# Reordering the first norm: whose features are loaded first, and at which projection slices the tiles of blocks 2 and 3 are made

## The chip, the cores and the metric

One Trainium2 chip, one of its cores. The metric is the device time of one execution in microseconds (us); the kernel before takes 2851.79 us (median of 3 runs, 2849.84 to 2853.08). All arithmetic that is seen here is in float32; a matmul of full precision is made of three, from high and low halves of its operands.

## The reference, cut to what matters

One transformer layer over 2048 tokens of width 1024. Only the beginning of it matters here: the first norm and the projections of the stick-breaking attention that read its result.

```python
mod_all = einsum('bd,lde->lbe', silu(c), ada_w) + ada_b
h = rms_norm(x, norm_g[0]) * (1 + sc_m) + sh_m     # the first norm, modulated
qkv = (h @ w_qkv).reshape(b, s, 3, 16, 64)
for q0 in range(0, s, 128):                        # stick-breaking attention
    z = q[q0:q0+128] @ k[:q0+128].T * scale
    sp = where(mask, softplus(z), 0); rest = reverse_cumsum(sp)
    a = where(mask, exp(z - rest), 0)
    out[q0:q0+128] = a @ v[:q0+128]
x = x + gate * rms_norm(out @ w_o, norm_g[1])      # then a SwiGLU FFN with its own norms
```

## The kernel before, in words

The 2048 tokens are four blocks (0 to 3) of 512, and the 16 heads are eight pairs. `project` (L429) makes keys, queries and values of one pair for one block. A product is eight **slices**, k = 0 to 7, one for each 128 of the 1024 features, and each slice is three matmuls (`mm3`, L169 to L173). The products come in the order keys (t = 1), queries (t = 0), values (t = 2), so "keys k4" below is slice 4 of the keys. `STEPS` (L33) has the steps in order: pair 0 of block 0, pair 1 of block 0 (the parked step), then pair 0 of blocks 1, 2 and 3, then pair 1 and so on. Between the slices `project_to` (L561) and the main loop put the stages of the attention: scores (`z`, L580), two sigmoids (L597, L599), a scan that breaks the sticks (`w`, L609 and L614), a product on GpSimd (`a`, L621), transposes (`t`, L631), a split of the turned tile in high and low (`aT`, L641 on ScalarE, L647 on VectorE), and the product with the values (`o`, L659). The scores have three PSUM buffers: the fourth score tile waits until the scan has read the first. The turned tiles have two.

The **first norm** of blocks 1 to 3 is woven into the projection of the block ahead of each:

- `x_load` (L304) fetches a block's x by tokens, four loads of 512 KB. `x_square` (L322) makes a tile's sum of squares on ScalarE (L162), the mean on VectorE (L164) and the power on GpSimd (L166). `x_spread` (L336) and `x_share` (L342) turn the four columns into a row that all features use.
- `cols_load` (L316) fetches the same block by features from `xt`, four loads of 512 KB (`xc`), two features' tiles in each.
- `first_norm` (L396) makes tile k of a block: `scale_cols` (L361) multiplies by the row, on VectorE for even k (L365) and on GpSimd for odd k (L369), two tiles ahead of the rest; `modulate` (L371) adds the shift and splits. An even tile costs one ScalarE instruction (L376) and one on VectorE (L377). An odd tile costs two on ScalarE (L381, L382) and one on VectorE (L384), or on GpSimd for block 3. After each odd tile the pair is stored (`h_s`, L407), for the other heads.

TensorE, ScalarE, VectorE and GpSimd each run their instructions in the order in which the Python issues them (the manual schedule). SyncE (SP) issues all loads and stores, from one queue whose order the framework's scheduler decides; each DMA also waits until the eighth one ahead of it has landed.

So the places of the calls in the loop over slices are the order of the queues. Before the change: block 3's x is loaded in the parked step's values k0, block 2's features at block 1's keys k0, block 3's features at block 2's keys k0. Block 3's squares stand in block 1's step at queries k2 and k7 and values k1 and k7 (`SQUARE_AT`, L73), and the first four tiles of a block in the step ahead of it at queries k4 and k6 and values k3 and k5 (`NORM_AT`, L75). The other four are made at the first slices of the block's own keys.

Of the kernel before, what the change touches and what calls it, by code (L numbers as in the profile page):

```python
# [69 lines left out]

H2_STEP = 3

SQUARE_AT = [(0, 2), (0, 7), (2, 1), (2, 7)]  # L73

NORM_AT = [(0, 4), (0, 6), (2, 3), (2, 5)]  # L75

LAST_HELD = 30

def f32(ap):
    return ap.bitcast(F32)  # L80
# [22 lines left out]
def hybrid_trunk_kernel(  # L103
# [55 lines left out]
    def rms_scale(pool, src, tag, junk):  # L159

        ssq = pool.tile([P, 1], F32, name=f"{tag}_ssq", tag="rms_ssq", bufs=10)
        nc.scalar.activation(junk, src, AF.Square, accum_out=ssq)  # L162
        ms = pool.tile([P, 1], F32, name=f"{tag}_ms", tag="rms_ms", bufs=4)
        nc.vector.tensor_scalar(ms, ssq, 1.0 / D, EPS, op0=ALU.mult, op1=ALU.add)  # L164
        rstd = pool.tile([P, 1], F32, name=f"{tag}_rstd", tag="rms_rstd", bufs=4)
        nc.gpsimd.tensor_tensor(rstd, ms, mhalf, op=ALU.pow)  # L166
        return rstd
# [136 lines left out]
    def x_load(b):  # L304
        for i in range(4):
            r0 = b * BT + i * P
            if b == 2:
                if i % 2 == 0:
                    pair = att.tile([P, 2, D], F32, name=f"x{b}_{i}", tag="qt", bufs=BUFS["qt"])
                tok = pair[:, i % 2]  # L310
            else:
                tok = att.tile([P, D], F32, name=f"x{b}_{i}", tag="v", bufs=BUFS["v"])
            nc.sync.dma_start(tok, x[r0 : r0 + P])
            x_tiles[b, i] = tok

    def cols_load(b):  # L316
        for m in range(KC // 2):
            cols = att.tile([P, 2, BT], F32, name=f"xc{b}_{m}", tag="kt", bufs=BUFS["kt"])
            nc.sync.dma_start(cols, xt[b - 1, :, 2 * m : 2 * m + 2])
            x_cols[b, 2 * m], x_cols[b, 2 * m + 1] = cols[:, 0], cols[:, 1]  # L320

    def x_square(b, i):  # L322
        if b > 0:
            tok = x_tiles[b, i]
            x_rstd[b, i] = rms_scale(att, tok, f"n0_{b}_{i}", junk=tok)
            return
        xn = att.tile([P, D], F32, name=f"xn{b}_{i}", tag="kt", bufs=BUFS["kt"])
        x_norm[b, i] = xn
        x_rstd[b, i] = rms_scale(att, x_tiles[b, i], f"n0_{b}_{i}", junk=xn)
# [66 lines left out]
    def first_norm(b, k):  # L396
        if b is None or k >= KC:
            return
        if k % 2 == 0:
            ht = att.tile([P, 2, 2, BT], F32R, name=f"ht0_{b}_{k // 2}", tag="ht", bufs=BUFS["ht"])  # L400
            norm_h.setdefault(b, []).extend([ht[:, 0], ht[:, 1]])
            norm_tile[b] = ht
        for ahead in range(0 if k == 0 else k + 2, min(k + 3, KC)):
            scale_cols(b, ahead)
        modulate(norm_h[b][k], b, k)
        if k % 2 == 1:
            nc.sync.dma_start(h_s[b][:, k - 1 : k + 1], f32(norm_tile[b]))  # L407
# [21 lines left out]
    def project(at):  # L429

        p, b = STEPS[at]
        begun = (p, b) == (0, 0)
        early, parked = (p, b) in EARLY, (p, b) == PARKED

        nb = STEPS[at + 1][1] if at + 1 < len(STEPS) and STEPS[at + 1][0] == 0 else None
        if STEPS[at] == (PARKED[0], 1):
            unpark()
        h = norm_h[b] if p == 0 or parked else h_load(p, b)

        def product(t):  # L440
            if begun:
                return first_acc[t]
            w = weights[p, t]
            if parked and t == 1:
                acc = zps.tile([P, BT], F32, name=f"pj{p}_{b}_{t}", tag="z")
            else:
                acc = accps.tile([P, BT], F32, name=f"pj{p}_{b}_{t}", tag="acc")
            ahead = b == NB - 1 and p + 1 < NPAIR
            for k in range(KC):
                if t == 1:  # L450
                    if p == 0:
                        first_norm(b, k + 4)
                    if k == 0 and nb and nb > 1:
                        cols_load(nb)
                    if k == 5 and waiting:
                        waiting.pop()()
                if parked and t == 1 and k % 2 == 0:
                    nc.sync.dma_start(*stores[k // 2])
                if parked and (t, k) == (1, 6):
                    split_early(1, 2, ["whl"])  # L460
                if nb == 1 and t == 1 and k < 4:
                    x_square(nb, k)
                if nb and t == 1 and 2 <= k < 6:
                    x_spread(nb, k - 2)
                if nb == 1 and (t, k) == (2, 0):
                    x_load(3)
                if nb in (1, 2) and (t, k) in SQUARE_AT:
                    x_square(nb + 1, SQUARE_AT.index((t, k)))
                if nb and (t, k) == (0, 1):
                    x_share(nb)  # L470
                if (t, k) in NORM_AT:
                    first_norm(nb, NORM_AT.index((t, k)))
                if ahead and k == 0:
                    load_weights(p + 1, t)
                if ahead and k == 6:
                    split_weights(p + 1, t)
                mm3(acc, (w[0][:, k], w[1][:, k]), (h[k][:, 0], h[k][:, 1]), k == 0, k == KC - 1)
                yield
            return acc

        def split(acc, tag):
            hl = att.tile([P, 2, BT], F32R, name=f"{tag}n{p}_{b}", tag="qkn", bufs=BUFS["qkn"])
            nc.scalar.copy(hl[:, 0], acc)
            nc.vector.tensor_tensor(hl[:, 1], acc, f32(hl[:, 0]), op=ALU.subtract)
            return hl

        closing = (p, b) == (NPAIR - 1, NB - 1)
        if closing:
            wo_load(0, 0, "whl")
            wo_load(0, 1, "ht")  # L490
        n = split((yield from product(1)), "k")
        if closing:
            wo_load(0, 2, "whl")
        if parked:
            nc.sync.dma_start(k_park, f32(n))
        else:
            kt = att.tile([P, 2, BT], F32R, name=f"kt{p}_{b}", tag="kt", bufs=BUFS["kt"])
            for e in range(2):
                for part in range(2):
                    nc.sync.dma_start(  # L500
                        f32(kt[part * HD : (part + 1) * HD, e]), f32(n[e * HD : (e + 1) * HD, part])
                    )
            keys[p, b] = kt

        n = split((yield from product(0)), "q")
        if closing:
            wo_load(0, 3, "whl")
        if parked:
            nc.sync.dma_start(q_park, f32(n))
        else:  # L510
            qt = att.tile([P, 2, 2, BT], F32R, name=f"qt{p}_{b}", tag="qt", bufs=BUFS["qt"])
            for e in range(2):
                for half in range(2):
                    nc.sync.dma_start(
                        f32(qt[half * HD : (half + 1) * HD, e]), f32(n[e * HD : (e + 1) * HD])
                    )
            queries[p, b] = qt

        acc = yield from product(2)
        tag = "w" if early else "tmp"  # L520
        vT = att.tile([P, BT], F32, name=f"vT{p}_{b}", tag=tag, bufs=BUFS[tag])
        nc.scalar.copy(vT, acc)

        def values_turn():
            pool, ptag = (zps, "z") if early else (accps, "acc")
            pt = pool.tile([P, 4, 2, HD], F32, name=f"vt{p}_{b}", tag=ptag)
            for i in range(4):
                nc.tensor.transpose(
                    pt[:, i].rearrange("p e d -> p (e d)"), vT[:, i * P : (i + 1) * P], ident
                )  # L530
            v = att.tile([P, 4, 2, 2, HD], F32R, name=f"v{p}_{b}", tag="v", bufs=BUFS["v"])
            nc.scalar.copy(v[:, :, :, 0], pt)
            nc.vector.tensor_tensor(v[:, :, :, 1], pt, f32(v[:, :, :, 0]), op=ALU.subtract)
            if parked:
                nc.sync.dma_start(v_park, f32(v))
            else:
                values[p, b] = v

        if early:
            waiting.append(values_turn)  # L540
            return
        for _ in range(VGAP):
            yield
        values_turn()
# [911 lines left out]
    for n, (s, f) in enumerate(groups):  # L1456
# [3 lines left out]
        for at, product in enumerate(PRODUCTS):  # L1460
            acc = banks_of[{1: 0, 6: 0, 7: 0, 4: 0, 5: 1, 3: 1, 2: 2}[product]]
            for k in range(H4):
# [4 lines left out]
                t = 4 * at + k  # L1467
# [193 lines left out]
```

## Time and profile before

| what | value |
|---|---|
| median of 3 runs | 2851.79 us (2849.84 to 2853.08) |
| the profiled execution | 2850.27 us |
| its span, first to last instruction | 2848.1 us |
| TensorE busy | 2791.3 us, 98% of the span |
| VectorE / ScalarE / GpSimd busy | 2024.3 / 1636.4 / 1293.5 us |
| mean granted TensorE clock | 0.998 |

The profiled execution's own time is 2850.27 us: 2.2 us of it lie outside the span. Rows of the trace have the start in us from the span's beginning, the duration, the engine, the line of the kernel, the tiles (out<-in), and in brackets the idle time of the engine just before and what ended it. PE is TensorE, DVE VectorE, ACT ScalarE, POOL GpSimd, SPq the queue of SyncE. In rows with three numbers and slashes these are minimum, median and maximum in ns.

### The profile page before, as it was taken

What the parts mean: (1) busy time and instruction counts of PE and PEld (TensorE: products, weight loads), DVE (VectorE), ACT (ScalarE), POOL (GpSimd) and SP (SyncE); (2) the same over time, 40 slices, a digit from 0 to 9 for tenths busy, and PEclk for the clock granted to TensorE, in tenths of its full rate; (3) what the DMA queues carried; (4) which work ended last, traced back from release to release, by engine and by line L of the source; (5) the groups of instructions that cost most, each with busy time, mean ns of one, the idle gap of its engine ahead of it and who ended that gap; (6) DMA issues with size and microseconds to landing.
All of it is one profiled execution on the core that took longest, in us unless ns stands there. A gap on an engine that the chain in (4) does not pass through costs nothing.

```text
span 2848.1 us, 41654 instructions
## 1 busy us (share of the span) xinstructions
PE 2791.3 (98%) x13764; PEld 2327.7 (82%) x13764; DVE 2024.3 (71%) x2817; ACT 1636.4 (57%) x3278; POOL 1293.5 (45%) x2040
## 2 busy tenths in 40 slices
PE   7899999999999999999999999999999999999998
PEld 6688888888888888887888888888788888888887
DVE  6788898888888888888866766655776655133367
ACT  5787877788787877777645533333433333322243
POOL 1575666666575655657410122221222222544454
PEclk9999999999999999999999999999999999999999
DMA  9865546657565635546288644334453335545575
GB/s 367 312 213 172 189 149 233 208 171 235 184 211 193 205 121 179 198 131 232 83 304 308 207 137 152 122 94 160 135 170 115 111 100 171 191 133 154 180 230 187
DMA packets 241095, 523.12 MB, mean 184 GB/s; under 512 B 22512, under 2 KB 110576, under 8 KB 223216
## 3 DMA queue, kind: packets, MB, share of 16 engines
q1 hardware_dynamic: 240880, 520.47, 56.1%
q8 instruction: 108, 1.77, 0.3%
q14 instruction: 107, 0.88, 0.1%
HBM read 353.14 MB, written 118.49 MB: 166 GB/s over the span
## 4 chain that ended last, share of the span: by engine, by line
PE 86%; DVE 5%; DMA 3%; ACT 2%; issue 2%; POOL 1%; SPq 0%; DVEq 0%; ACTq 0%; POOLq 0%
PE s L171 9%; PE s L172 9%; PE s L173 9%; PE z L580 8%; PE o L659 8%; PE t L631 8%; PE pj L171 5%; PE pj L173 5%; PE pj L172 5%; PE o L171 5%; PE o L173 5%; PE o L172 5%; PE y L173 1%; PE y L171 1%; PE y L172 1%
## 5 line engine op out<-in xcount | busy, mean ns | idle before, releaser
L621 POOL TENSOR_TENSOR a<-a,w 128x512 f32<-128x512 f32 (+3 forms) x640 | 619.9, 969 | 211.5 <-DVE w L614 127.1
L614 DVE TENSOR_TENSOR_SCAN w<-z,c,begin 128x512 f32<-128x512 f32 x384 | 489.2, 1279 | 81.7 <-ACT z L599 60.2
L171 PE MATMUL s<-r,l 128*128 128x512 f32 x1232 | 482.2, 391 | 4.3 <-DVE p L1423 3.9
L173 PE MATMUL s<-r,l 128*128 128x512 f32 x1232 | 480.0, 390 | 0.0
L172 PE MATMUL s<-r,l 128*128 128x512 f32 x1232 | 480.0, 390 | 0.0
L597 ACT ACTIVATE a<-z 128x512 f32<-128x512 f32 (+3 forms) x640 | 347.1, 542 | 167.0 <-PE z L580 135.2
L659 PE MATMUL o<-aT,v 128*128 128x512 f32 (+3 forms) x1280 | 384.3, 381 | 0.1
L647 DVE TENSOR_TENSOR aT<-t,aT 128x512 fp32r<-128x512 f32 (+3 forms) x640 | 358.9, 594 | 22.8 <-ACT aT L641 22.2
L580 PE MATMUL z<-kt,qt 128*128 128x512 f32 (+3 forms) x1280 | 363.8, 365 | 6.2 <-DVE w L609 6.2
L641 ACT CAST aT<-t 128x512 fp32r<-128x512 f32 (+3 forms) x640 | 314.3, 534 | 73.5 <-PE t L631 63.5
L599 ACT ACTIVATE z<-z 128x512 f32<-128x512 f32 (+3 forms) x640 | 345.5, 540 | 0.0
L1431 POOL TENSOR_TENSOR one<-p,p 128x512 f32<-128x512 f32 x44 | 71.5, 1624 | 578.6 <-issue 321.9
L171 PE MATMUL pj<-ht,w 128*128 128x512 f32 x768 | 308.8, 402 | 5.7 <-issue 1.4
L631 PE MATMUL t<-begin,a 128*128 128x128 f32 x2176 | 295.2, 273 | 13.4 <-DVE aT L647 10.3
L631 PEld LDWEIGHTS t<-begin,a 128*128 128x128 f32 x2176 | 255.0, 140 | 63.4 <-DVE aT L647 14.1
L172 PE MATMUL pj<-ht,w 128*128 128x512 f32 x768 | 302.8, 394 | 1.6 <-DVE ht L767 0.7
L173 PE MATMUL pj<-ht,w 128*128 128x512 f32 x768 | 302.6, 394 | 0.0
L171 PEld LDWEIGHTS s<-r,l 128*128 128x128 f32 x1232 | 231.5, 188 | 55.2 <-ACT l L1284 2.9
L173 PEld LDWEIGHTS s<-r,l 128*128 128x128 f32 x1232 | 231.7, 188 | 48.2
L172 PEld LDWEIGHTS s<-r,l 128*128 128x128 f32 x1232 | 231.7, 188 | 48.1 <-issue 0.5
L580 PEld LDWEIGHTS z<-kt,qt 128*128 128x128 f32 x1280 | 230.7, 189 | 44.2 <-DVE w L609 7.1
L609 DVE TENSOR_TENSOR_SCAN w<-z,begin 128x128 f32<-128x128 f32 (+3 forms) x256 | 208.7, 818 | 77.8 <-ACT z L599 64.9
(170 smaller groups left out, 4860.7 us busy)
## 6 DMA issues: line engine op xcount, KB each, us to landing
ht<-h_s SPq DMA_DIRECT2D x108, 1024.0 KB, 8.2
wi<-in_win SPq DMA_DIRECT2D x86, 512.0 KB, 3.9
qt<-qn SPq DMA_DIRECT2D x124, 256.0 KB, 4.9
ol_qt<-act_s SPq DMA_DIRECT2D x56, 512.0 KB, 3.8
act_s<-S SPq DMA_DIRECT2D x66, 256.0 KB, 4.0
br<-in_wout SPq DMA_DIRECT2D x66, 256.0 KB, 3.7
h_s<-ht SPq DMA_DIRECT2D x16, 1024.0 KB, 10.2
o_s<-os SPq DMA_DIRECT2D x128, 128.0 KB, 2.7
```

What stands on the lines that cost most here:

```text
L171: nc.tensor.matmul(acc, lhs[0], rhs[0], start=first, stop=False, **kw)
L172: nc.tensor.matmul(acc, lhs[0], rhs[1], start=False, stop=False, **kw)
L173: nc.tensor.matmul(acc, lhs[1], rhs[0], start=False, stop=last, **kw)
L580: nc.tensor.matmul(z[:, :n], q[:, e, part, r * P : (r + 1) * P], k[:, e, :n], start=part == 0, stop=part == 1,)
L597: nc.scalar.activation(a[:, :n], z[:, :n], AF.Sigmoid, scale=QK_SCALE)
L599: nc.scalar.activation(z[:, :n], z[:, :n], AF.Sigmoid, scale=-QK_SCALE)
L614: nc.vector.tensor_tensor_scan(rest[:, rev], left[:, rev], begin[:, :BT][:, rev], initial=carries[r], op0=ALU.mult, op1=ALU.bypass,)
L621: nc.gpsimd.tensor_tensor(a[:, :n], a[:, :n], rest[:, 1 : n + 1], op=ALU.mult)
L631: nc.tensor.transpose(pt[:, rb * P : (rb + 1) * P], weighed[i, rb][:, j * P : (j + 1) * P], ident)
L641: nc.scalar.copy(hl[:, 0, t0:], pt[:, t0:])
L647: nc.vector.tensor_tensor(hl[:, 1, t0:], pt[:, t0:], f32(hl[:, 0, t0:]), op=ALU.subtract)
L659: nc.tensor.matmul(acc[:, t0:], lhs, hl[:, part, t0:], start=sc == qb and j == 0 and part == 0, stop=sc == 0 and j == 3 and part == 1,)
```

## The change

Loads: in the parked step's values k0, block 2's features are loaded in place of block 3's x. Block 3's x is loaded at block 1's keys k0, where block 2's features were. Block 3's features are loaded at block 1's values k0, in place of block 2's keys k0.

Squares: those of block 3 move to block 1's values k0, k2, k4 and k6. Those of block 2 stay.

Tiles: block 1's stay. Of blocks 2 and 3, three tiles (0, 1, 2) are made in the step ahead, at values k2, k4 and k6, and the other five at k0 to k4 of the block's own keys.

```diff
-SQUARE_AT = [(0, 2), (0, 7), (2, 1), (2, 7)]
+SQUARE_AT = {1: [(0, 2), (0, 7), (2, 1), (2, 7)], 2: [(2, 0), (2, 2), (2, 4), (2, 6)]}
 
-NORM_AT = [(0, 4), (0, 6), (2, 3), (2, 5)]
+NORM_AT = {
+    None: [], 1: [(0, 4), (0, 6), (2, 3), (2, 5)],
+    2: [(2, 2), (2, 4), (2, 6)], 3: [(2, 2), (2, 4), (2, 6)],
+}
...
                     if p == 0:
-                        first_norm(b, k + 4)
-                    if k == 0 and nb and nb > 1:
-                        cols_load(nb)
+                        first_norm(b, k + (4 if b == 1 else 3))
+                    if k == 0 and nb == 2:
+                        x_load(3)
...
-                if nb == 1 and (t, k) == (2, 0):
-                    x_load(3)
-                if nb in (1, 2) and (t, k) in SQUARE_AT:
-                    x_square(nb + 1, SQUARE_AT.index((t, k)))
+                if nb in (1, 2) and (t, k) == (2, 0):
+                    cols_load(nb + 1)
+                if nb in (1, 2) and (t, k) in SQUARE_AT[nb]:
+                    x_square(nb + 1, SQUARE_AT[nb].index((t, k)))
                 if nb and (t, k) == (0, 1):
                     x_share(nb)
-                if (t, k) in NORM_AT:
-                    first_norm(nb, NORM_AT.index((t, k)))
+                if (t, k) in NORM_AT[nb]:
+                    first_norm(nb, NORM_AT[nb].index((t, k)))
```

`nb` is the block of the next step, if that step is of pair 0.

## The prediction

> **What bounds the kernel now.** I read the page first, for TensorE's share; then the waits of PE, cut at 150 us; then busy time by stretch, cut where the products begin and end; and last the rows of each engine around the one long gap.
>
> ```profile
> PE 2791.3 (98%) x13764; PEld 2327.7 (82%) x13764; DVE 2024.3 (71%) x2817; ACT 1636.4 (57%) x3278; POOL 1293.5 (45%) x2040
> ```
> ```profile
> PE z L580 <- DVE w L609: 6.2, 1, 6.2
> PE t L631 <- DVE aT L647: 4.2, 4, 1.3
> PE t L631 <- POOL w L594: 1.7, 1, 1.7
> PE vt L528 <- ACT vT L522: 1.3, 1, 1.3
> ```
> ```profile
> 88.50:94.90 6.40, 0.21 (x2) 0.02 (x1) 5.81 (x9) 5.92 (x13) 3.61 (x5) 0.91 1.01 422
> 94.90:98.20 3.30, 1.95 (x6) 1.24 (x7) 1.45 (x4) 3.26 (x8) 3.15 (x5) 0.50 1.05 408
> 98.20:108.60 10.40, 9.76 (x42) 7.25 (x41) 9.15 (x13) 7.28 (x16) 4.76 (x9) 0.89 0.93 297
> 108.60:118.20 9.60, 9.60 (x54) 8.04 (x53) 8.27 (x14) 5.83 (x15) 6.87 (x13) 1.00 0.98 369
> 118.20:130.90 12.70, 10.63 (x55) 8.40 (x54) 11.16 (x15) 12.16 (x26) 8.53 (x14) 1.00 0.80 251
> 136.60:150.00 13.40, 11.14 (x60) 9.06 (x59) 11.17 (x14) 12.24 (x23) 9.02 (x13) 1.00 0.50 186
> 150.00:250.00 100.00, 100.00 (x549) 85.19 (x548) 85.07 (x106) 80.44 (x167) 65.18 (x139) 1.00 0.61 192
> ```
>
> TensorE is the bound for the whole span. The second fence holds its waits from 60 to 150 us (total, times, longest). The stretches (length, then busy PE, PEld, DVE, ACT, POOL, granted clock, DMA share, GB/s) show where: block 1's values end at 88.5, then comes a gap, then block 2's keys from 98.2, queries from 108.6, values from 118.2, block 3's keys from 136.6. From 150 to 250 PE is busy in 100 of 100 us. So whatever the change does must be done before 150, and a shift there reaches the end one for one. What is there to win is small: 6.2 + 1.3 us for the gap, 4.2 + 1.7 in the small waits after it, some slow matmuls behind the gap (clock 0.50 and 0.89). The DMA share is 1.0 until 98: the loads land when bandwidth lets them.
>
> The gap itself:
>
> ```profile
> 78.81 1.06 ACT L162 ACTIVATE x<-x 128x1024 f32<-128x1024 f32 x1 [0.58 <-DMA x<-in_x]
> 79.78 0.19 ACT L162 ACTIVATION_READ_ACCUMULATOR x<-x 128x1 f32 x1
> ```
> ```profile
> 87.02 0.75 DVE L365 SCALAR_TENSOR_TENSOR xc<-xc,g_eff,x 128x512 f32<-128x512 f32 x1 [6.87 <-DMA xc<-in_xt]
> 88.30 1.17 DVE L365 SCALAR_TENSOR_TENSOR xc<-xc,g_eff,x 128x512 f32<-128x512 f32 x1 [0.52 <-DMA xc<-in_xt]
> 89.39 1.75 DVE L377 SCALAR_TENSOR_TENSOR ht<-xc,shift,ht 128x512 fp32r<-128x512 f32 x1
> 94.41 0.42 DVE L609 TENSOR_TENSOR_SCAN w<-z,begin 128x128 f32<-128x128 f32 x1
> ```
> ```profile
> 94.88 1.22 PE L580 MATMUL z<-kt,qt 128*128 128x512 f32 x2 [6.19 <-DVE w L609]
> 97.44 1.11 PE L528 MATMUL vt<-begin,vT 128*128 128x128 f32 x4 [1.35 <-ACT vT L522]
> ```
>
> Block 2's features land at 87.0 and 88.3. VectorE stood at the first of them for 6.87 us, and the sigmoids and the scan of the first attention unit were queued behind. PE's fourth score tile needs that scan (94.41 + 0.42 = 94.83) and starts at 94.88.
>
> **The change part by part.** No instruction is added or taken away, and the build's order shows TensorE's unchanged. Only queues differ.
>
> (1) The loads. Block 2's features go where block 3's x was in SP's queue, and the x where the features were:
>
> ```profile
> L313 SPq DMA_DIRECT2D x<-in_x x4: 1178/1206/1231, 67.5 to 71.4; - x4
> DMA to landing us min/median/max: 11.2/11.5/11.9
> ```
> ```profile
> L319 SPq DMA_DIRECT2D xc<-in_xt x4: 328/328/1167, 74.0 to 78.8; - x4
> DMA to landing us min/median/max: 12.5/12.7/13.0
> ```
>
> Both are four loads of 512 KB with the same DMAs ahead, so they trade landings: the features land by 71.4 + 11.9 = 83.3, the x lands its four tiles at 87.0, 88.3, then at the latest 78.8 + 12.7 = 91.5 (estimates from these rows).
>
> (2) What stands there then. The features are no longer late, but block 3's squares now come first: ScalarE's new order is the split of the queries, squares 0 and 1, the high half of tile 0 (L376), square 2, tile 1 (L381, L382), the first sigmoids. VectorE has both means (L164) ahead of tile 0's scaling, and GpSimd both powers (L166) ahead of tile 1's. So the same sigmoids now stand behind the x's second tile.
>
> ```profile
> L365 DVE SCALAR_TENSOR_TENSOR xc<-xc,g_eff,x x11: 737/749/1557, 60.8 to 125.0; 128x512 f32<-128x512 f32 x11
> L376 ACT ACTIVATE ht<-xc,shift x10: 710/722/786, 61.6 to 123.5; 128x512 fp32r<-128x512 f32 x10
> L369 POOL TENSOR_TENSOR xc<-xc,x x10: 1295/1734/1816, 61.9 to 118.0; 128x512 f32<-128x512 f32 x10
> L377 DVE SCALAR_TENSOR_TENSOR ht<-xc,shift,ht x9: 740/752/1754, 62.3 to 115.3; 128x512 fp32r<-128x512 f32 x9
> L381 ACT ACTIVATE xc<-xc,shift,g_eff x9: 802/813/817, 63.4 to 117.3; 128x512 f32<-128x512 f32 x9
> L382 ACT CAST ht<-xc x9: 618/620/622, 64.2 to 118.1; 128x512 fp32r<-128x512 f32 x9
> L384 DVE TENSOR_TENSOR ht<-xc,ht x8: 659/692/1201, 64.9 to 107.3; 128x512 fp32r<-128x512 f32 x8
> ```
> ```profile
> 93.01 0.15 DVE L164 TENSOR_SCALAR n_ms<-n_ssq 128x1 f32<-128x1 f32 x1 [0.36 <-ACT x L162]
> ```
> ```profile
> 93.31 0.92 POOL L166 TENSOR_TENSOR n_rstd<-n_ms,mhalf 128x1 f32<-128x1 f32 x1 [0.81 <-DVE n_ms L164]
> ```
> ```profile
> 93.66 0.27 ACT L599 ACTIVATE z<-z 128x128 f32<-128x128 f32 x1
> ```
>
> The chain: landing 88.3, square and readout 1.25 (89.55), mean, and power by 0.30 + 0.92 after the mean's start (90.8), L369 1.73 (92.5), L381 0.81 and L382 0.62 (93.9), two sigmoids of 0.27 (94.5). VectorE's L384 0.69 fits beside the sigmoids (94.6), the scan 0.42: 95.0. ScalarE's rows overlap by some 0.1 us each, so 94.6 is as likely. Against 94.83 that is -0.2 to +0.2; with L384 at its longest +0.7. **I take 0: the wait stays and changes its owner**, from the features to the x. Behind it ScalarE has square 3 (1.06), L376 (0.72), two sigmoids and the copy that the values' transposes need, where it now has L381, L382, the same sigmoids, square 3 and that copy: 0.7 less. I take -0.4 for block 2's first key slice, 97.8 instead of 98.2.
>
> (3) Block 2's keys, one tile fewer in stock.
>
> ```profile
> 98.60 0.59 ACT L532 CAST v<-vt 128x512 fp32r<-128x512 f32 x1 [0.43 <-PE vt L528]
> ```
> ```profile
> 101.29 1.21 DVE L609 TENSOR_TENSOR_SCAN w<-z,begin 128x512 f32<-128x512 f32 x1
> ```
> ```profile
> 102.82 0.39 PE L172 MATMUL pj<-ht,w 128*128 128x512 f32 x1
> ```
>
> PE wants the low half of tile 4 at 102.8, less 0.4. VectorE's order puts it behind the fourth scan and a scaling. Ahead of that scan ScalarE now has L381 and L382 after its cast at 98.60, where it had L376: +0.71 against -0.4, within the slack to 101.29. So the scan ends at about 102.4, L365 at 103.1, L377 at 103.9, or 104.9 if it takes its longest 1.75: a wait of 1.4 to 2.4 us at k4. Tile 6 follows over a spread and a scan, 0 to 1.2 more. The present waits at k7, about 0.6, go. With the -0.4: +0.4 to +2.6, and -0.9 if the x lands 1.3 us sooner after its issue, as in its old place. I take **+0.8**, near +0.4, as most L377 are at their median.
>
> (4) Block 2's queries lose tiles 0 and 1 of block 3. PE is busy 9.60 of 9.60 there, so nothing is won inside; but the queues arrive emptier, and two waits of VectorE's splits just behind (about 0.7 of the 4.2) should go: **-0.7**, ends -0.7 and 0.
>
> (5) Block 2's values gain them. ScalarE is busy 12.16 of 12.70 there, and gets L376, L381, L382 and gives one L381, L382 to block 3's keys: +0.72. VectorE gets two L365 and one L377, +2.25. PE's transposes have two buffers that VectorE's splits free.
>
> ```profile
> 127.47 0.55 PE L631 MATMUL t<-begin,a 128*128 128x128 f32 x3 [1.31 <-DVE aT L647]
> 134.97 0.77 PE L631 MATMUL t<-begin,a 128*128 128x128 f32 x5 [1.66 <-POOL w L594]
> ```
>
> Following the new order, the split that frees the second buffer comes some 2 us late near 131, and the wait at 134.97, which now ends with GpSimd, takes in 1.4 of it: **+0.6**, ends 0 and 0.72 + 2.25 = +3.0.
>
> (6) Block 3's keys make five tiles instead of four: ScalarE +1.43 in a stretch where it is busy 12.24 of 13.40; GpSimd +2.6.
>
> ```profile
> 141.34 0.18 POOL L620 COPY c<-w 128x1 f32<-128x1 f32 x1 [4.11 <-DVE w L609]
> ```
>
> GpSimd's part fits into these 4.11 us; ScalarE's doesn't all, and the last low half is behind one more product of GpSimd: **+1.2**, ends 0 and 1.43 + 1.3 = +2.7.
>
> (7) The rest costs nothing. Block 3's features move up, from block 2's keys k0 to block 1's values k0, behind the queries' copies, while their first use moves back into block 2's values: more slack at both ends. Block 2's first store stands behind three of these loads; its buffer is wanted only in block 2's values. Near 131 to 170 the scheduler moves weight loads ahead of stores and of block 3's queries; PE has no wait there. If these covers failed, VectorE would wait for features as it does now at 87.
>
> Sum: 0 + 0.8 - 0.7 + 0.6 + 1.2 = **+1.9 us**. The profiled execution took 2850.27 (span 2848.1 and 2.2 around it), so 2852.2; the median shown is 1.5 higher, so 2853.7 on its scale. The terms' ends that can go together give -2 to +5.
>
> One rule speaks against the change. The Trainium skill, SBUF — State Buffer, "Who interferes with whom", has VectorE instructions with two SBUF inputs and GpSimd instructions that read SBUF lock each other out. The trace agrees: L377 took 1.75 at 89.39, its median being 0.75, while GpSimd scaled tiles. By that rule three more such instructions beside GpSimd would each lose 1.0 us, an estimate that makes the sum +4.9.
>
> **The rivals.**
>
> *A, faster: the first scan is no longer held.* If the x landed by 82, the scan would follow block 1's values at once: 6.2 + 1.3 gone, and up to 2.0 of slow matmuls (half of the 1.95 at clock 0.50, 0.11 of the 9.76 at 0.89), then 1 to 3 given back at block 2's keys, where PE would outrun the tiles: -6.5 to -8.5, so 2843 to 2845. For it: the x landed 1.3 us faster than the features. Against it: that is 1.3 us, not 6, and DMA share is 1.0 on both sides. Chance 0.13. The Trainium skill, TensorE: Matmul & The Clock Gate, Part 1, says that an idle window of about 3.4 us halves the clock; the 0.50 agrees, and by it those matmuls are won only if the gap falls below that.
>
> *B, slower: the splits fall behind in block 2's values.* Terms 3, 5 and 6 at their ends, +2.6 + 3.0 + 2.7 = +8.3, less term 4's 0.7 and what the ends share: +6 to +8, so 2858 to 2860. It decides when a split near 131 is later than the 1.66 us that PE waits anyway, so that each scan starts late and the next unit inherits it. For it: ScalarE's 12.16 of 12.70. Against it: DVE idles 1.5 in that stretch. Chance 0.17.
>
> *C, a small gain.* The x lands 1.3 faster, term 3 is 0 and the waits of term 4 go: -1 to -4, so 2848 to 2851. Chance 0.08.
>
> That the change doesn't do what it says is no rival: SP's order in the build has the loads where the diff puts them.
>
> **How the numbers follow.** My forecast has 0.62, its own range -2 to +5: 2850 to 2857. I call 0.2%, 5.7 us, no change, about what a measurement of this kernel can tell. Forecast and C lie within it: same 0.70; A faster 0.13, B slower 0.17. The range from 2845 to 2860 holds forecast, C and B, 0.87, and reaches A's edge.
>
> **What would show it.** Right: ScalarE's first square of block 3 waits for DMA until about 87, the fourth score tile starts at 94 to 96, a wait for L377 appears at block 2's key k4, PE is full from 150 on. Wrong: a square of block 3 that starts at 79 to 83, a score gap under 3 us (A), or waits on L647 over 6 us between 118 and 150 (B).

## Result, and the profile after

| | before | after |
|---|---|---|
| median | 2852.31 us (2849.27 to 2854.36, 12 runs) | 2858.95 us (2857.17 to 2860.66, 12 runs) |
| span of the profiled execution | 2848.1 us | 2857.2 us |
| mean granted TensorE clock | 0.998 | 0.996 |

The ratio of after to before is 1.0023, interval 1.0014 to 1.0032: between 4.0 and 9.1 us slower. The predicted 2853.7 was 5.2 too low. The range from 2845 to 2860 holds the time, but the forecast's own range, 2850 to 2857, does not: the time lies where only rival B reached. Whether it is more than the 5.7 us that the prediction called no change stays open, as the interval has both.

Line numbers of after are three higher than those of before behind `NORM_AT` (L75). The first two views answer to the prediction's first two: the page's busy times, then TensorE's waits from 60 to 160 us (total, times, longest).

```profile
PE 2795.6 (98%) x13764; PEld 2330.5 (82%) x13764; DVE 2032.9 (71%) x2817; ACT 1638.1 (57%) x3278; POOL 1296.4 (45%) x2040
```
```profile
PE z L583 <- DVE n_ms L167: 8.6, 1, 8.6
PE t L634 <- DVE aT L650: 5.9, 4, 2.3
PE pj L175 <- DVE ht L380: 2.6, 3, 2.2
PE pj L175 <- DVE ht L387: 0.7, 2, 0.4
PE pj L175 <- POOL ht L387: 0.2, 1, 0.2
```

The gap ahead of the fourth score tile is 8.6 us and no longer 6.2. The 1.3 for `vt` and the 1.7 for GpSimd are gone; 2.6 for L380 are new, and the splits cost 5.9 where they cost 4.2. The row names the tiny mean L167 as the one that ended the gap, because it is the instruction that VectorE finished last; what TensorE needed was the scan just before it (below).

**Where the time went.** TensorE's order is the same in both kernels, so the same score tile can be looked up in both, and the distance between two such tiles is free of what an execution lost before. Here are five of them, before and then after. They are a tile of block 1's values, the first in block 2's keys, the first in block 2's values, the first in block 3's keys after slice k0, and one near the end of the disturbed stretch.

```profile
85.87 0.40 PE L580 MATMUL z<-kt,qt 128*128 128x256 f32 x2
...
99.64 0.52 PE L580 MATMUL z<-kt,qt 128*128 128x128 f32 x2
...
119.04 0.68 PE L580 MATMUL z<-kt,qt 128*128 128x512 f32 x2
...
137.59 0.68 PE L580 MATMUL z<-kt,qt 128*128 128x512 f32 x2
...
156.24 0.68 PE L580 MATMUL z<-kt,qt 128*128 128x512 f32 x2
```
```profile
86.08 0.40 PE L583 MATMUL z<-kt,qt 128*128 128x256 f32 x2
...
100.82 0.52 PE L583 MATMUL z<-kt,qt 128*128 128x128 f32 x2
...
122.07 0.68 PE L583 MATMUL z<-kt,qt 128*128 128x512 f32 x2
...
141.90 0.68 PE L583 MATMUL z<-kt,qt 128*128 128x512 f32 x2
...
161.75 0.68 PE L583 MATMUL z<-kt,qt 128*128 128x512 f32 x2
```

The four distances were 13.77, 19.40, 18.55 and 18.65 us; they are 14.74, 21.25, 19.83 and 19.85. So the **gap** costs 0.97 more, block 2's **keys and queries** 1.85, its **values** 1.28, and block 3's **keys** 1.20: 5.30 in all. That lies inside the interval of the medians. The spans differ by 9.1; the other 3.8 arise ahead of the first tile (0.2) and behind the last (3.6, most of it after 2400 us), where the change touches nothing, and single executions of the kernel before differ by 5 us among themselves (2849.27 to 2854.36). So the experiments below are read by these four distances, with the medians as a check.

From there on TensorE is full, as it was from 150 before (length, busy PE, PEld, DVE, ACT, POOL, granted clock, DMA share, GB/s):

```profile
156.00:256.00 100.00, 99.97 (x548) 85.04 (x549) 85.41 (x107) 80.94 (x168) 65.14 (x140) 1.00 0.57 182
```

**The gap.** Rows of ScalarE, GpSimd, VectorE and TensorE of after around it:

```profile
88.42 1.06 ACT L165 ACTIVATE x<-x 128x1024 f32<-128x1024 f32 x1 [5.19 <-DMA x<-in_x]
...
90.22 1.06 ACT L165 ACTIVATE x<-x 128x1024 f32<-128x1024 f32 x1 [0.64 <-DMA x<-in_x]
```
```profile
95.27 1.27 POOL L372 TENSOR_TENSOR xc<-xc,x 128x512 f32<-128x512 f32 x1
```
```profile
95.53 1.56 DVE L387 TENSOR_TENSOR ht<-xc,ht 128x512 fp32r<-128x512 f32 x1 [0.92 <-ACT ht L385]
97.01 0.41 DVE L612 TENSOR_TENSOR_SCAN w<-z,begin 128x128 f32<-128x128 f32 x1
```
```profile
97.47 1.22 PE L583 MATMUL z<-kt,qt 128*128 128x512 f32 x2 [8.57 <-DVE n_ms L167]
```

The wait is where the prediction put it, on the x's first two tiles. But they start at 88.42 and 90.22, not at 87.0 and 88.3. The low half L387 takes 1.56 where its median before was 0.69, beside GpSimd's scaling of a tile. The scan ends at 97.42, not at 95.0.

The view of the two load lines shows why the x is late (issue durations, first and last issue; then DMA to landing, minimum, median, maximum). First the x, then the features:

```profile
L316 SPq DMA_DIRECT2D x<-in_x x4: 327/328/1197, 74.2 to 80.6; - x4
...
DMA to landing us min/median/max: 12.1/14.0/14.3
```
```profile
L322 SPq DMA_DIRECT2D xc<-in_xt x4: 1152/1206/1254, 67.8 to 71.7; - x4
...
DMA to landing us min/median/max: 12.8/12.9/13.1
```

The features need 12.9 us where the x needed 11.5 in the same place, and the x behind them needs 14.0 where the features needed 12.7, with the last issue at 80.6 and not at 78.8. The loads did not trade landings: the second one lost 1.3. Why loads by features take longer than loads by tokens is not shown.

**The values.** Two stretches between the same two score tiles in block 2's values, first before, then after:

```profile
128.09:135.82 7.73, 6.07 (x39) 5.12 (x38) 6.31 (x10) 5.51 (x15) 6.91 (x13) 1.00 0.42 138
```
```profile
130.20:140.13 9.93, 7.65 (x39) 6.51 (x38) 7.91 (x12) 7.36 (x18) 8.26 (x14) 0.83 0.51 182
```
```profile
135.87 0.33 PE L634 MATMUL t<-begin,a 128*128 128x128 f32 x1 [2.28 <-DVE aT L650]
```

The stretch is 2.20 longer. TensorE idles 9.93 - 7.65 = 2.28 in it, all in the one wait of the row, where it idled 1.66: 0.62 more. The other 1.58 are busy time: the same matmuls at a granted clock of 0.83 in place of 1.00.

**Block 3's keys.** Here the sum of the idle time hardly moves (18.65 - 16.39 = 2.26 before, 19.85 - 17.48 = 2.37 after), at a granted clock of 1.00 in both. The starts of the matmuls show the loss. Where slices follow each other without a wait, the starts are 0.23 apart; at two low halves that GpSimd makes they are 0.48 and 0.61 behind the matmul ahead, and the next matmul 0.33 and 0.34 behind them: 0.84 of the 1.20. The second of them:

```profile
154.64 0.39 PE L174 MATMUL pj<-ht,w 128*128 128x512 f32 x1
155.25 0.50 PE L175 MATMUL pj<-ht,w 128*128 128x512 f32 x1 [0.22 <-POOL ht L387]
```

### The profile page after: what moved, and what is told of

It is laid out like the page before. It is cut to its first block, busy times and chain, and to the rows that moved or that the text cites. A ratio compares the mean times of both kernels' runs of the same rounds, so it can differ in the third digit from the quotient of the medians.

```text
span 2857.2 us, 41657 instructions
## 1 busy us (share of the span) xinstructions
PE 2795.6 (98%) x13764; PEld 2330.5 (82%) x13764; DVE 2032.9 (71%) x2817; ACT 1638.1 (57%) x3278; POOL 1296.4 (45%) x2040
## 3 DMA queue, kind: packets, MB, share of 16 engines
q8 instruction: 108, 1.77, 0.3%
## 4 chain that ended last, share of the span: by engine, by line
PE 86%; DVE 5%; issue 3%; ACT 3%; DMA 2%; POOL 1%; SPq 0%; DVEq 0%; POOLq 0%; ACTq 0%
PE s L174 9%; PE s L176 9%; PE s L175 9%; PE z L583 8%; PE o L662 8%; PE t L634 8%; PE pj L174 6%; PE pj L175 5%; PE pj L176 5%; PE o L176 4%; PE o L175 4%; PE o L174 4%; PE y L176 2%; PE y L174 2%; PE y L175 2%
## 5 line engine op out<-in xcount | busy, mean ns | idle before, releaser
L650 DVE TENSOR_TENSOR aT<-t,aT 128x512 fp32r<-128x512 f32 (+3 forms) x640 | 358.9, 595 | 24.0 <-ACT aT L644 23.3
```

The costliest lines, as they stand in the source:

```text
L650: nc.vector.tensor_tensor(hl[:, 1, t0:], pt[:, t0:], f32(hl[:, 0, t0:]), op=ALU.subtract)
```

## The experiments

All by the distances between the five score tiles, as change against before in us, and by medians; each median of before was measured beside that of the run. Each kernel has one trace. In e1, e5, e6 and e10 the four transposes of block 3's row come four slices later on TensorE, within "keys, queries"; elsewhere its order is unchanged.

| kernel | gap | keys, queries | values | block 3's keys | sum | median us, before us | ratio (interval) |
|---|---|---|---|---|---|---|---|
| after | +0.97 | +1.85 | +1.28 | +1.20 | +5.30 | 2858.95, 2852.31 | 1.0023 (1.0014 to 1.0032) |
| e1 | -9.08 | +4.10 | +1.16 | +1.22 | -2.60 | 2848.7, 2851.89 | 0.9990 (0.9981 to 0.9999) |
| e2 | +0.42 | +2.95 | -0.47 | +0.02 | +2.92 | 2855.22, 2851.89 | 1.0013 (1.0004 to 1.0022) |
| e3 | +1.73 | +0.03 | +1.28 | +1.23 | +4.27 | 2856.6, 2851.89 | 1.0018 (1.0009 to 1.0027) |
| e4 | +5.19 | +0.02 | +0.02 | +0.02 | +5.25 | 2857.74, 2851.89 | 1.0020 (1.0011 to 1.0030) |
| e5 | -8.50 | +3.87 | +0.12 | 0.00 | -4.51 | 2848.14, 2852.17 | 0.9986 (0.9977 to 0.9995) |
| e6 | -8.49 | +3.77 | +1.42 | +1.24 | -2.06 | 2848.76, 2852.17 | 0.9987 (0.9978 to 0.9996) |
| e7 | +0.90 | +2.73 | -2.11 | +1.26 | +2.78 | 2852.99, 2852.17 | 1.0002 (0.9993 to 1.0011) |
| e8 | +0.77 | +2.05 | +0.29 | +1.26 | +4.37 | 2857.1, 2852.17 | 1.0015 (1.0006 to 1.0023) |
| e9 | -2.52 | +1.85 | +1.29 | +1.24 | +1.86 | 2854.95, 2851.9 | 1.0011 (1.0002 to 1.002) |
| e10 | -8.50 | +3.77 | +1.13 | +0.01 | -3.59 | 2849.36, 2851.9 | 0.9992 (0.9984 to 1.0001) |

All the sums lie inside the intervals of their ratios. The theory is that the loss has four places that are separate: the x lands late and holds the scan; block 2's keys lack a tile; block 2's values make tiles 0 to 2 of block 3 in place of 2 and 3, with five scalings in place of two; block 3's keys have one tile too many. The main rival puts it in one place, from which the rest is inherited.

**e1: block 3's squares, late.** The loads and tiles stay as changed; the squares go behind the first scans, to block 2's keys k5 and k7 and queries k1 and k2, and the row that is made of them with them.

```diff
-SQUARE_AT = {1: [(0, 2), (0, 7), (2, 1), (2, 7)], 2: [(2, 0), (2, 2), (2, 4), (2, 6)]}
+SQUARE_AT = {1: [(0, 2), (0, 7), (2, 1), (2, 7)], 3: [(1, 5), (1, 7), (0, 1), (0, 2)]}
+
+SPREAD_AT = {1: [(1, 2), (1, 3), (1, 4), (1, 5)], 2: [(1, 2), (1, 3), (1, 4), (1, 5)], 3: [(1, 7), (0, 1), (0, 3), (0, 4)]}
+
+SHARE_AT = {1: (0, 1), 2: (0, 1), 3: (0, 5)}
...
-                if nb and t == 1 and 2 <= k < 6:
-                    x_spread(nb, k - 2)
+                if nb and (t, k) in SPREAD_AT[nb]:
+                    x_spread(nb, SPREAD_AT[nb].index((t, k)))
...
-                if nb in (1, 2) and (t, k) in SQUARE_AT[nb]:
-                    x_square(nb + 1, SQUARE_AT[nb].index((t, k)))
-                if nb and (t, k) == (0, 1):
+                if nb in (1, 3) and (t, k) in SQUARE_AT[nb]:
+                    x_square(2 if nb == 1 else 3, SQUARE_AT[nb].index((t, k)))
+                if nb and (t, k) == SHARE_AT[nb]:
                     x_share(nb)
```

> The changed kernel, with block 3's squares moved behind the first scans (block 2's keys k5 and k7, queries k1 and k2), and their spreads and the row after them (row at queries k5). Theory (the first scan waits for block 3's x, 8.6 us in the changed kernel): the fourth score tile starts by 90 instead of 97.5, and the gap shrinks from 8.6 to under 2 us. Some of it comes back in block 2's keys, whose tiles are made at one per some 1.4 us: 4 to 6 us faster than the changed kernel, 2852 to 2855 when that is at 2859, so level with the kernel before or up to 3 us faster. Rival (bandwidth or the elementwise work of this stretch is the bound, and the order only says where the wait shows): the score gap goes, but block 2's keys end at the same 111 to 112 us as in the changed kernel, and the time stays within 2 us of 2859.

The gap is gone: 4.69 us from the first score tile to the second, at a granted clock of 1.00, where before it took 13.77 at 0.78. The two windows, e1's and then before's:

```profile
85.70:90.39 4.69, 4.47 (x24) 3.52 (x22) 3.60 (x7) 3.97 (x11) 1.47 (x4) 1.00 1.04 422
```
```profile
85.87:99.64 13.77, 6.24 (x24) 4.49 (x22) 9.53 (x15) 10.92 (x22) 8.74 (x12) 0.78 1.02 413
```

Of the 9.08, 1.77 are busy time (6.24 - 4.47), the rest idle time. So the features do land in time, and the squares, which stood waiting for the x, made the gap of after. But 4.10 are given back at once in block 2's keys and queries, where TensorE now waits for low halves:

```profile
93.76 0.50 PE L179 MATMUL pj<-ht,w 128*128 128x512 f32 x1 [1.16 <-DVE ht L391]
...
97.04 0.80 PE L179 MATMUL pj<-ht,w 128*128 128x512 f32 x1 [2.32 <-DVE ht L384]
```

Even so the median, 2848.7, is below the theory's 2852 to 2855: the kernel is faster than after, and just faster than before.

**e2: block 3's tiles at their old places.**

```diff
-    2: [(2, 2), (2, 4), (2, 6)], 3: [(2, 2), (2, 4), (2, 6)],
+    2: [(2, 2), (2, 4), (2, 6)], 3: [(0, 4), (0, 6), (2, 3), (2, 5)],
-                        first_norm(b, k + (4 if b == 1 else 3))
+                        first_norm(b, k + (3 if b == 2 else 4))
```

> The changed kernel with block 3's first four tiles back at their old places (queries k4, k6, values k3, k5; the others four slices ahead). Loads, squares and block 2's tiles stay changed. Theory: the loss behind 118 us (block 2's values and block 3's keys, some 3 us of the 5.3 that stand at 160 us in the profile) goes, the score gap of 8.6 and the wait at k4 of block 2's keys (2.2) stay: 2 to 3 us faster than the changed kernel, about 2856. Rival (the late waits only pass on what the gap lost): no more than 1 us faster.

The losses in block 2's values and in block 3's keys go (-0.47 and +0.02): 2.93 less than in after. The keys and queries lose 1.10 more, ahead of block 3's tiles: the granted clock is 0.91 over them where after has 0.97, and busy time 19.65 where it has 18.45 (what the clock hangs on stands under e8). With 0.55 less in the gap, the sum is 2.4 below after's 5.30.

**e3: four tiles of block 2 ahead**, at block 1's values k1, k3, k5 and k7.

```diff
-    2: [(2, 2), (2, 4), (2, 6)], 3: [(2, 2), (2, 4), (2, 6)],
+    2: [(2, 1), (2, 3), (2, 5), (2, 7)], 3: [(2, 2), (2, 4), (2, 6)],
-                        first_norm(b, k + (4 if b == 1 else 3))
+                        first_norm(b, k + (3 if b == 3 else 4))
```

> The changed kernel with four tiles of block 2 made ahead instead of three (values k1, k3, k5, k7; the others four slices ahead). Theory: the wait of 2.2 us for tile 4's low half at k4 of block 2's keys goes, the score gap stays at 8 to 9.5 us since the first tile's place is only one slice earlier: 1 to 2.5 us faster than the changed kernel. Rival (VectorE's and ScalarE's work there is full, and a tile made earlier holds up the scan as long): the gap grows by what the wait at k4 gives, no difference.

Keys and queries lose nothing any more (+0.03), and the wait for L380 shrinks from 2.6 to this row:

```profile
PE pj L175 <- DVE ht L380: 0.2, 1, 0.2
```

The values' loss stays at 1.28 and block 3's at 1.23, so neither is inherited from block 2's keys. The gap grows by 0.76: ScalarE makes tile 3 (0.80 and 0.62 us) ahead of the copy for the values' transposes, and TensorE waits 2.3 for that copy.

**e4: the loads alone.** The kernel before, with only block 3's x and block 2's features exchanged.

```diff
-                    if k == 0 and nb and nb > 1:
-                        cols_load(nb)
+                    if k == 0 and nb == 2:
+                        x_load(3)
+                    if k == 0 and nb == 3:
+                        cols_load(3)
...
-                    x_load(3)
+                    cols_load(2)
```

> The kernel before with one part of the change: block 2's features are loaded in the place of block 3's x and the x in theirs. Squares and tiles stay at their old places, block 3's features too. Theory (the wait changes its owner): ScalarE now stands on the x at the first square, at queries k2, about 88 to 90, and the score gap is 6 to 9 us: 0 to +4 us against the kernel before. Rival (the features were what was late, and the loads alone cure it): the score gap falls below 3 us and the time by 4 us or more.

+5.25 us, all of it in the gap, more than the theory's range. ScalarE then TensorE:

```profile
90.39 1.06 ACT L162 ACTIVATE x<-x 128x1024 f32<-128x1024 f32 x1 [12.11 <-DMA x<-in_x]
```
```profile
PE z L582 <- DVE w L611: 11.4, 1, 11.4
```

The squares stand at block 1's queries k2 there, so ScalarE stands 12.11 us for an x that lands at 90.4, and everything behind it is late. With the squares ahead of the scan, the exchange takes no wait away; in e1, with the squares behind it, it does.

**e5: e1, with four tiles of block 2 and block 3's tiles near their old places.** This is the version to which e1 to e3 point.

```diff
-    2: [(2, 2), (2, 4), (2, 6)], 3: [(2, 2), (2, 4), (2, 6)],
+    2: [(2, 1), (2, 3), (2, 5), (2, 7)], 3: [(0, 6), (2, 1), (2, 3), (2, 5)],
-                        first_norm(b, k + (4 if b == 1 else 3))
+                        first_norm(b, k + 4)
```

> The version of e1 (loads as changed, block 3's squares late) with four tiles of block 2 made ahead (values k1, k3, k5, k7) and block 3's tiles near their old places (queries k6, values k1, k3, k5). Theory: the three losses are separate and add. e1 took 2848.7; taking a fourth tile of block 2 ahead should be worth the 2.1 us of block 2's keys, block 3's old places the 2.9 us that e2 (2855.2) lay below a changed kernel of 2858.95, less about 1 for the queries: 2844 to 2846, with no wait over 1 us for a low half in block 2's keys, and under 3 us of waits for the splits in block 2's values. Rival: once the score gap is gone VectorE and GpSimd are the bound of block 2's step, so that what one place gives another takes: 2847 to 2850.

It is faster than both kernels, 0.9986 of before. The values and block 3's keys lose nothing. But the keys and queries still give back 3.87. TensorE idles 3.9 in them (92.61 to 115.88): 1.7 at a score tile for DMA, 1.4 in five waits for halves of tiles, none over 0.7, and the rest for a scan and for block 3's row. The time lies where the rival put it: with the gap gone, the losses no longer add.

```profile
PE z L587 <- DMA xc<-in_xt: 1.7, 1, 1.7
PE pj L178 <- ACT ht L389: 0.7, 1, 0.7
```

**e6: e5 with block 3's tiles where the change put them.**

```diff
-    2: [(2, 1), (2, 3), (2, 5), (2, 7)], 3: [(0, 6), (2, 1), (2, 3), (2, 5)],
+    2: [(2, 1), (2, 3), (2, 5), (2, 7)], 3: [(2, 2), (2, 4), (2, 6)],
-                        first_norm(b, k + 4)
+                        first_norm(b, k + (3 if b == 3 else 4))
```

> e5 with block 3's tiles where the change put them (values k2, k4, k6, five in block 3's own keys). Theory: it lies 1 to 3 us above e5, all of it between 118 and 150 us, and about 2 below e1: 2846 to 2848. Rival: the loss in block 2's values came from the tiles that block 2's keys had left over, and not from block 3's; then it equals e5 within 0.5 us.

By the score tiles it is 2.45 behind e5, all in the values (1.42 for 0.12) and block 3's keys (1.24 for 0.00), as the theory has it. The medians, 2848.76 and 2848.14, don't separate the two. But it isn't the 2 us below e1 that the theory asked for: the sums are -2.06 and -2.60, and the fourth tile of block 2, worth 1.82 in e3, gains 0.33 in the keys and queries here.

**e7: the changed kernel with block 3's three tiles early**, at queries k4 and k6 and values k3.

```diff
-    2: [(2, 2), (2, 4), (2, 6)], 3: [(2, 2), (2, 4), (2, 6)],
+    2: [(2, 2), (2, 4), (2, 6)], 3: [(0, 4), (0, 6), (2, 3)],
```

> The changed kernel with block 3's three tiles made at queries k4 and k6 and values k3, so two of them left out of block 2's values; block 3's keys still make five. Theory (the tiles in block 2's values cost 2.2 to 3.0, the queries without them gain 0.9, block 3's keys cost 1.2): 1.3 to 2.1 us below the changed kernel, 2857 to 2858, the waits for the splits in block 2's values back near 4 us. Rival: the five tiles in block 3's keys carry the loss and not the values: no change, 2859.

The values gain 3.39 against after (-2.11 for +1.28), the keys and queries lose 0.88 (granted clock 0.92, and busy time 19.31 for 18.45), and block 3's five tiles still cost 1.26 in its keys: 2.52 in all, a little over the theory's 2.1; the median fell by more than that (2852.99), which stays open. The stretch of the values that took 9.93 in after, here:

```profile
133.67:139.73 6.06, 6.06 (x39) 5.11 (x37) 5.62 (x10) 5.15 (x14) 4.33 (x11) 1.00 0.49 120
```

TensorE doesn't wait in it at all, not even the 1.66 of before, and the clock is 1.00.

**e8: one low half on GpSimd**, that of block 2's tile 1 (the 1.56 us of VectorE ahead of the scan).

```diff
-            eng = nc.gpsimd if b == NB - 1 else nc.vector
+            eng = nc.gpsimd if b == NB - 1 or (b, k) == (2, 1) else nc.vector
```

> The changed kernel with the low half of block 2's tile 1 made on GpSimd. In the changed kernel that instruction took 1.56 us on VectorE (median 0.69) ahead of the first scan, beside GpSimd's scaling of a tile. Theory: without it the first scan ends 1.3 to 1.7 us sooner, so the fourth score tile waits about 7.1 in place of 8.6 us, and the end moves by half or all of that: 2857.3 to 2858.5. Rival: GpSimd's added product of some 1.5 us only moves the delay to tile 3, which waits for GpSimd at block 2's keys k3: score gap shorter, but 2859 again.

The score tile waits 7.25 and not 8.57, as expected, but the next instruction of TensorE then waits for ScalarE's copy:

```profile
95.72 1.22 PE L583 MATMUL z<-kt,qt 128*128 128x512 f32 x2 [7.25 <-DVE w L612]
98.00 1.12 PE L531 MATMUL vt<-begin,vT 128*128 128x128 f32 x4 [1.05 <-ACT vT L525]
```

So the gap is only 0.20 shorter, and the keys lose that again. By the score tiles the kernel is 0.93 below after all the same, in the values, and not for the theory's reason: the same wait of 2.28 stands there as in after, but the clock stays at 1.00.

```profile
129.78:138.70 8.92, 6.54 (x38) 4.95 (x37) 7.84 (x12) 7.31 (x18) 7.76 (x13) 1.00 0.46 161
```

Busy time is 6.54 against 7.65 in after's stretch: 1.11 of after's loss in the values was the clock.

The traces show why the same wait lowers the clock in one kernel and not in the other. In all twelve, from 60 to 2790 us, the granted clock falls to 0.50 for 3.41 us or a whole multiple of it (6.83 in the gap of before, 10.24 in that of after). Counted in steps of 3.41 us from there, after's wait lies whole in one step, and the next step has the low clock; e8's is cut in two, 0.82 and 1.56 of idle time with what little else stands there (length less busy time):

```profile
132.71:136.12 3.41, 1.13 (x7) 0.63 (x6) 3.41 (x5) 2.54 (x7) 3.33 (x4) 1.00 0.37 154
136.12:139.53 3.41, 3.41 (x14) 3.13 (x13) 2.40 (x5) 1.71 (x5) 2.51 (x9) 0.50 0.95 303
```
```profile
130.57:133.98 3.41, 2.59 (x15) 1.86 (x13) 3.18 (x3) 3.41 (x10) 3.41 (x4) 1.00 0.00 0
133.98:137.39 3.41, 1.85 (x10) 1.35 (x11) 3.41 (x8) 1.87 (x7) 2.60 (x4) 1.00 0.84 327
137.39:140.80 3.41, 3.41 (x23) 2.85 (x24) 2.52 (x5) 2.35 (x5) 3.27 (x11) 1.00 0.65 211
```

Over the same stretch every such step at full clock with at most 1.80 us of idle time is followed by full clock, and every one with 1.88 or more by half. The extra busy time of e2 and e7 in the keys has the same origin: steps with 2.09 and 2.24 idle, then 0.50 from 109.5 and 109.8. So where a wait falls among the steps decides about some 1 us here; no kernel was traced twice, so whether it falls the same way in another execution is not shown.

**e9: the x right behind the features**, so that a store of 1 MB stands behind the x in SP's queue and not ahead.

```diff
-                    if k == 0 and nb == 2:
-                        x_load(3)
...
                 if nb in (1, 2) and (t, k) == (2, 0):
                     cols_load(nb + 1)
+                    if nb == 1:
+                        x_load(3)
```

> The changed kernel with block 3's x loaded right behind block 2's features, so that one store of 1 MB stands behind the x and no longer ahead of it. Theory (the score gap is set by the landing of the x's second tile): the store took 1.3 us of SP's queue, and 1 MB at some 410 GB/s is 2.6 us of transfer, so the second square starts 1.3 to 2.6 us before 90.22, the fourth score tile's wait falls from 8.6 to 6.0 to 7.3, and the kernel ends 1 to 2 us below 2858.95. Rival: what holds the scan is work behind the square on three engines (the mean, the power, the tile's scaling beside the low half), which fills up whatever is gained: wait over 8 us, no change.

The squares start at 85.92 and 87.20 in place of 88.42 and 90.22; this execution was 0.47 later than after's at the first score tile, so they are 3.0 and 3.5 sooner, and the second no longer waits for its load.

```profile
85.92 1.06 ACT L165 ACTIVATE x<-x 128x1024 f32<-128x1024 f32 x1 [2.22 <-DMA x<-in_x]
...
87.20 1.06 ACT L165 ACTIVATE x<-x 128x1024 f32<-128x1024 f32 x1
```
```profile
PE z L583 <- DVE n_ms L167: 5.1, 1, 5.1
```

The wait fell by 3.5, the gap by 3.49 (-2.52 for +0.97), the whole by 3.44; the other three distances didn't move. With e1 that settles what the gap hangs on: the x's landing, one for one. It is more than the 1.3 to 2.6 that the theory asked for; the rival is refuted.

**e10: e5 with block 3's features loaded later**, at block 2's keys k0.

```diff
-                if nb in (1, 2) and (t, k) == (2, 0):
-                    cols_load(nb + 1)
+                if nb == 1 and (t, k) == (2, 0):
+                    cols_load(2)
...
+                    if k == 0 and nb == 3:
+                        cols_load(3)
```

> e5 with block 3's features loaded at block 2's keys k0, as before the change, and not at block 1's values k0. In e5 TensorE stood 1.7 us at 105.5 for the queries' DMAs, which run beside these loads. Theory: once the score gap is gone those DMAs are late next, and without the 2 MB beside them the 1.7 us go: 2846 to 2847.5. Rival: the queries' DMAs are late because SP issues them after 94.9 behind the keys', whatever follows them: same as e5, 2848, or up to 2 worse where block 3's features are then late at queries k6.

Of the 1.7 for DMA 0.2 are left, and nothing is won in the keys and queries (3.77 for e5's 3.87): a split is 1.2 late in them instead (94.25 to 117.42). The values lose 1.13 where e5 lost 0.12, which stays open too.

```profile
PE t L640 <- DVE aT L656: 1.2, 1, 1.2
```

The theory fails: taking the DMA's wait away left the keys and queries as they were. What bounds block 2's keys and queries in e5 and e10, where all of VectorE, ScalarE and DMA take turns, stays open.

## Why the prediction was right, and where it was not

By its own steps. The terms were 0 and +0.8 for the gap and the keys together, then -0.7, +0.6, +1.2: +1.9. Measured were 0.97 + 1.85, then -0.92, +2.20, +1.20: +5.30. Of the 3.4 that are missing, 1.37 lie in the gap (the prediction had -0.4 for the keys behind it), 0.65 in block 2's keys and 1.60 in its values; term 4 won 0.22 more than foreseen. Of its four signs, the first square's wait (88.42), the wait at k4 and the full TensorE behind came; the fourth score tile, at 97.47, missed its 94 to 96. The places and the owners of the waits were right; wrong were the landing in step 1 and a duration in step 3, and the clock in step 5 was left out. That the range holds the time is luck: it reached to 2860 for rival B, whose mechanism did not come.

1. *The loads trade landings.* Right for the features: no engine waits for them any more. Wrong for the x, by 1.4 and 1.9 us. The step took the place in the queue for the cause of the landing and each load for the same load. The trace of before, with 11.5 for the x in the first place and 12.7 for the features in the second, couldn't tell the two apart; after has 12.9 for the features in the first place.
2. *The wait stays and changes its owner.* Right, and shown by e1 (squares late: no gap) and e9 (x sooner: gap shorter by the same). The size was wrong: the scan ended 2.4 late, mostly by step 1, some 0.9 by the low half of 1.56. That ScalarE has less behind the scan was right, and undersized: 0.4 foreseen, 1.41 measured (the tile was 2.38 late, the next keys 0.97).
3. *Block 2's keys, one tile fewer.* The mechanism and the row were right, a wait of 1.4 to 2.4 at k4, but the choice of the low end was not. The instruction that had to be at its median was not:

```profile
104.89 1.57 DVE L380 SCALAR_TENSOR_TENSOR ht<-xc,shift,ht 128x512 fp32r<-128x512 f32 x1
```
```profile
106.52 0.50 PE L175 MATMUL pj<-ht,w 128*128 128x512 f32 x1 [2.23 <-DVE ht L380]
```

   In the trace of before the same kind of instruction had stood in about that place, and had been slow already:

```profile
103.01 1.58 DVE L377 SCALAR_TENSOR_TENSOR ht<-xc,shift,ht 128x512 fp32r<-128x512 f32 x1
```

   A median over all stages was taken where a row of the stage was to be had. e3 shows that the missing tile is the whole of this term.
4. *Block 2's queries, -0.7.* Right: the distance from 119.04 to 128.09 before and from 122.07 to 130.20 after is 9.05 and 8.13, so -0.92.
5. *Block 2's values, +0.6.* The wait was right to the tenth (2.28 for 1.66, +0.62): a split came 2.28 late where some 2 were foreseen, and took in all of the old wait where 1.4 of it were. The busy time behind it was left out, +1.58, of which e8 shows 1.11 to be the granted clock; the other 0.47 is not explained. e2 shows that it is the place of block 3's tiles that brings it on; e5, with three tiles in the values but tile 0 and its three scalings ahead of them, loses 0.12, although the clock falls once there too (0.50 from 124.8).
6. *Block 3's keys, +1.2.* Right, +1.20, and at the low halves of GpSimd as foreseen; e2, e5 and e10 take it away with the fifth tile. That it agrees to the tenth is luck, as the step gave only the ends 0 and 2.7 a working.
7. *The rest costs nothing.* Right within the stretch; TensorE is full behind it.

Of the rivals, A's condition (the scan not held) was not met, but e1 met it, and A's sizes of the gap hold there: 7.3 idle and 1.8 of slow matmuls won, against 7.5 and up to 2.0 foreseen. But 4.1 were given back in the keys and queries where A had 1 to 3, and with the losses behind them e1 ended at -2.6 and not at -6.5 to -8.5. B was nearer than the forecast in its total and in terms 3 and 5 at their upper ends, but its mechanism did not come: e3 and e7 show that the losses of the keys, the values and block 3's keys are not inherited from each other, and the waits at L650 are 4.7 between 118 and 150, under its mark of 6.

Two rules of the Trainium skill bear on it. The Trainium skill, SBUF — State Buffer, "Who interferes with whom", says that VectorE and GpSimd take turns at a shared port; the trace agrees with 1.56 at 95.53 beside GpSimd's 1.27 at 95.27, where the median before was 0.69. The +4.9 that the prediction worked out by it is near the 5.30, but that is luck: with that one delay away, in e8, the wait was 1.32 shorter, and only 0.20 of it was kept in the gap; the slow L380 at 104.89 is some 0.8 over its median; and what the x's landing and the clock cost is none of it. The Trainium skill, TensorE: Matmul & The Clock Gate, Part 1, describes a clock window that runs freely, whatever the kernel does. The trace agrees: one and the same wait of 2.28 us was followed by a lower clock in after and by a full one in e8, as the steps of 3.41 us cut it. But the prediction read from that Part that such a window has to be idle, and the traces show less to be enough: 1.88 us of idle time in 3.41.

## What to carry to other kernels

An exchange of two loads moves a wait from the user of the one to the user of the other: ask which instructions are queued behind the new one before asking how early the old one gets. Take the duration of an instruction from the row of the stage that it will stand in, not from its median over stages. And price a wait of TensorE with what follows it: 0.6 us more of waiting came with 1.1 us of lower clock, or with none, by where the wait fell.

## What the runs showed of the hardware

- Four loads of 512 KB by features took 12.9 us to landing where four by tokens had taken 11.5 in the same place, and the ones behind them 14.0 in place of 12.7. With a 1 MB store moved from ahead of the x to behind it, the squares that need the x began 3.0 and 3.5 us sooner (after and e9), more than the 1.3 us that the store held SP's queue.
- A wait of TensorE well under the gap of 6 to 9 us can lower the clock: 2.28 us did in after, and the same 2.28 in e8 did not. In the twelve traces, from 60 to 2790 us, the clock is granted in steps of 3.41 us: 1.88 us or more of idle TensorE within one step were followed by half the clock in the next, 1.80 or less by the full one.
- The instruction named as ending a wait can be the one that followed the cause on its engine: the mean L167, 0.12 us long, for the scan that ended at 97.42 (after).
